# Moving every tile of a hybrid decoder block to another address: two unused tiles at the ends of SBUF

## The chip, the cores and the metric

The kernel runs on one core of one Trainium2 chip. The metric is the device time of one execution in microseconds (us). The times before come from three runs; one further execution was recorded by the hardware profiler.

## What is computed

One layer of a decoder block on `x` of 1,024 rows by 1,024 channels, all in float32. Cut to what matters here:

```python
xn = rmsnorm(x, norm1_g)
qa, ka, va, qr, kr, vr, gr, gate_a, gate_b = split(xn @ w_in)       # 1024 x 12800
o_a = dilated_attention(rmsnorm(qa), rmsnorm(ka), va)                # 12 heads of 128, 3 groups of 4
o_r = head_groupnorm(retention(qr, kr, vr)) * silu(gr)               # 4 heads, chunks of 128 rows
y = sigmoid(gate_a) * (o_a @ w_proj_a) + sigmoid(gate_b) * (o_r @ w_proj_b)
x = x + y @ w_out
x = x + square(relu(rmsnorm(x, norm2_g) @ w_up)) @ w_down            # 1024 x 4096 x 1024
```

The attention groups look at every first, fourth and sixteenth row back in a window; their three outputs per slot are mixed by their softmax denominators. Retention carries a state from chunk to chunk with a decay per head.

## The kernel before

The kernel is one program of 18,158 instructions. Its large matrix products keep float32 accuracy by splitting each operand into a high part and a remainder, both held in a rounded 32-bit type (`R` in the code, `F` is plain float32), and by three matmuls for each product of two tiles:

```python
def mm(x, y, start, stop):
    self.nc.tensor.matmul(ps, x, y, start=start, stop=stop, skip_group_check=not first)   # line 193
...
mm(xh, yh, first and i == 0, False)
mm(xh, yl, False, False)
mm(xl, yh, False, i == n - 1)
```

The first operand is the stationary one (128 x 128, loaded into TensorE ahead of the matmul), the second is streamed through it, 384 or 512 columns at a time. All 9,780 matmuls of `R` data stand on line 193 (in `Pipe.group`), 2,304 of 384 columns and 7,476 of 512. Splitting a tile takes one ScalarE copy (line 287) and one VectorE subtraction (line 288).

The work goes through these stages, one after the other, with TensorE's order written out by hand:

- Attention: for each of 12 heads, eight row blocks of 128 rows; each takes 24 matmuls of 384 columns (query, key and value together; the rows of the normalised input are stationary, the weights are streamed), then transposes (line 607), scores (532), transposed probabilities (545) and values (552) in plain float32 (`F`). The rest of a block runs some steps later through a list of due functions (`Pipe.at`), so that TensorE has other matmuls meanwhile. `acc` (line 554) takes the output of a block, 128 values in rows of 130.
- Input products: gates, retention's queries and keys, its output gate, in seven products for eight (Strassen), on halves of 512 columns; `wh`/`wl` are stationary, `xh`/`xl` streamed.
- Retention: four heads, eight chunks each, with values (line 193), scores (769), a state update (`kzh`, `kzl`) and outputs (`vh`, `Sh`, `qh`, `smh`), transposes at 780 and 825.
- Projections of both mixers, with operands and gates reloaded from DRAM.
- The output product, the second norm and the transposes of its rows (line 958).
- The up product (Strassen again), whose squared-ReLU result goes to DRAM (`h_d`), and the down product, which reads it back as `h`, `xh`, `xl` and adds eight partial results into `Yd` (line 1109).

Weights come in by one class, `Weights`, with three or four raw buffers and six pairs of split buffers (`wh0` to `wh5`, `wl0` to `wl5`), each 4,096 bytes per partition. All transfers are issued by SyncE.

Where a tile lies is decided by pools. A pool grows either from the left end of SBUF upwards or, with `side="right"`, from the right end downwards; pools open and close in the order of the code, and a tile starts at a multiple of 32 bytes. The first left pool is `const`, so its content shifts every later left tile:

```python
const = pool(ctx, "const", 1)
rawp = pool(ctx, "rawp", 1)
wp = pool(ctx, "wp", 1)
big = pool(ctx, "big", 4)
...
half = const.tile([P, 2], F, name="half")
ident = const.tile([P, P], F, name="ident")
```

With this, the built program has `half` at byte 16512 of each partition, `ident` at 16544, `raw0` at 17120, `wh0` at 29408, the first `xh` of `big` at 78560, and on the right `bias` of attention at 175840 and `qT` at 177888. The streamed operand of each of the 9,780 matmuls begins 96 bytes past a multiple of 128.

Of the kernel before, what the change touches and what calls it, by code (L numbers as in the profile page):

```python
# [10 lines left out]
F = mybir.dt.float32  # L11
# [6 lines left out]
P = 128  # L18
# [219 lines left out]
def hybrid_block(ctx: ExitStack, tc: tile.TileContext, a: dict, out: bass.AP):  # L238
# [3 lines left out]
    def pool(stack, name, bufs, side="left", **kw):  # L242
        return stack.enter_context(tc.tile_pool(name=name, bufs=bufs, side=side, reuse_waits="tile", **kw))

    const = pool(ctx, "const", 1)
    rawp = pool(ctx, "rawp", 1)
    wp = pool(ctx, "wp", 1)
    big = pool(ctx, "big", 4)
# [959 lines left out]
```

## Time and profile before

| | us |
|---|---|
| median of 3 runs | 2324.09 (2323.64 to 2328.1) |
| profiled execution | 2327.33 |
| its span | 2325.6 |
| TensorE matmuls busy | 2281.0 (98%) |
| TensorE weight loads busy | 1952.9 (84%) |
| VectorE / ScalarE / GpSimd busy | 1165.8 / 926.2 / 104.0 |
| mean granted TensorE clock | 0.995 |
| HBM traffic | 303.19 MB, 130 GB/s over the span |

The profile lists instructions with their start and length. A matmul's length goes from its start to its modelled end and overlaps the next one, so the pace is read from the distance between starts, or from a piece of many matmuls in the chain of work that ended last. Weight loads overlap matmuls too.

### The profile page before, as it was taken

How to read it: one execution, taken by the hardware profiler on the slowest of the kernel's cores; microseconds unless marked ns; L12 is line 12 of the kernel's file. 1: busy time of each engine (PE TensorE's matmuls, PEld its weight loads, DVE VectorE, ACT ScalarE, POOL GpSimd, SP SyncE). 2: the span in 40 equal slices, each digit the busy share in tenths (PEclk: the TensorE clock that was granted, in tenths of full speed). 3: DMA queues.
4: the chain of work that ended last, by engine and by line, in shares of the span. 5: the costliest groups of instructions: out<-in, count | busy, mean ns of one | idle time of the engine just before them, and what ended most of it. 6: DMA issues, size and time to landing. Idle time of an engine off the chain costs nothing. (4 is left out here: it accounts for less than half of the span.)

```text
span 2325.6 us, 29822 instructions
## 1 busy us (share of the span) xinstructions
PE 2281.0 (98%) x11060; PEld 1952.9 (84%) x11060; DVE 1165.8 (50%) x2356; ACT 926.2 (40%) x2078; POOL 104.0 (4%) x148
## 2 busy tenths in 40 slices
PE   8999999999999999989999999999999999999999
PEld 7999998998888888868888878888788888888887
DVE  6344445454644445557676752363855555233532
ACT  6444444445343333335455533122566666211010
POOL 1111111110000000000000000000000000000000
PEclk9999999999999999999999999999999999999999
DMA  4212322332233333363433385554254457733601
GB/s 140 82 55 74 105 63 78 96 105 91 68 112 112 117 113 109 100 187 104 123 113 100 104 273 180 164 171 163 83 173 166 167 169 271 288 127 133 234 28 73
DMA packets 186275, 303.19 MB, mean 130 GB/s; under 512 B 13457, under 2 KB 99601, under 8 KB 182034
## 3 DMA queue, kind: packets, MB, share of 16 engines
q1 hardware_dynamic: 186130, 301.29, 39.9%
q8 instruction: 87, 1.43, 0.3%
q14 instruction: 58, 0.48, 0.1%
HBM read 204.68 MB, written 96.57 MB: 130 GB/s over the span
## 5 line engine op out<-in xcount | busy, mean ns | idle before, releaser
L193 PE MATMUL mm<-wh,xh 128*128 128x384 f32 (+1 forms) x1536 | 605.1, 394 | 5.1 <-ACT wh L287 5.1
L193 PE MATMUL mm<-wh,xl 128*128 128x384 f32 (+1 forms) x1536 | 561.7, 366 | 2.4 <-DVE xl L288 2.1
L288 DVE TENSOR_TENSOR wl<-raw,wh 128x1024 fp32r<-128x1024 f32 (+2 forms) x282 | 306.6, 1092 | 423.1 <-ACT wh L287 420.1
L193 PE MATMUL mm<-wl,xh 128*128 128x384 f32 (+1 forms) x1344 | 486.6, 362 | 2.6 <-DVE wl L288 2.6
L287 ACT ACTIVATE wh<-raw 128x1024 fp32r<-128x1024 f32 (+2 forms) x282 | 267.2, 953 | 535.7 <-PE mm L193 272.1
L193 PEld LDWEIGHTS mm<-wh,xh 128*128 128x128 f32 x1536 | 291.5, 190 | 36.6 <-ACT wh L287 5.7
L193 PEld LDWEIGHTS mm<-wh,xl 128*128 128x128 f32 x1536 | 290.4, 189 | 35.5 <-DVE xl L288 3.4
L193 PE MATMUL mm<-xl,wh 128*128 128x512 f32 x848 | 309.7, 390 | 1.7 <-DVE xl L288 1.7
L193 PE MATMUL mm<-xh,wh 128*128 128x512 f32 x848 | 310.1, 390 | 0.0
L193 PE MATMUL mm<-xh,wl 128*128 128x512 f32 x720 | 280.7, 390 | 0.0
L193 PEld LDWEIGHTS mm<-wl,xh 128*128 128x128 f32 x1344 | 256.3, 191 | 24.8 <-DVE wl L288 3.1
L193 PE MATMUL ms<-xh,wh 128*128 128x512 f32 x604 | 238.6, 395 | 3.9 <-DVE s L888 3.8
L193 PE MATMUL ms<-xh,wl 128*128 128x512 f32 x604 | 235.4, 390 | 0.0
L193 PE MATMUL ms<-xl,wh 128*128 128x512 f32 x604 | 235.3, 390 | 0.0
L193 PEld LDWEIGHTS mm<-xl,wh 128*128 128x128 f32 x848 | 159.5, 188 | 35.2 <-DVE xl L288 2.1
L193 PEld LDWEIGHTS mm<-xh,wh 128*128 128x128 f32 x848 | 159.6, 188 | 33.0
L1109 DVE TENSOR_TENSOR Yd<-Yd,mm 128x512 f32<-128x512 f32 x112 | 76.9, 686 | 172.3 <-PE mm L193 172.0
L193 PEld LDWEIGHTS mm<-xh,wl 128*128 128x128 f32 x720 | 135.4, 188 | 28.1
L193 PEld LDWEIGHTS ms<-xh,wh 128*128 128x128 f32 x604 | 113.5, 188 | 30.1 <-DVE s L888 4.2
L193 PEld LDWEIGHTS ms<-xh,wl 128*128 128x128 f32 x604 | 113.4, 188 | 23.8
L193 PEld LDWEIGHTS ms<-xl,wh 128*128 128x128 f32 x604 | 113.5, 188 | 22.4
L539 ACT ACTIVATE pr<-s,acc 128x128 f32<-128x128 f32 (+1 forms) x96 | 43.1, 449 | 149.2 <-DVE acc L537 136.9
(187 smaller groups left out, 2756.4 us busy)
## 6 DMA issues: line engine op xcount, KB each, us to landing
h_d<-hs SPq DMA_DIRECT2D x64, 512.0 KB, 3.9
raw<-in_w_att SPq DMA_DIRECT2D x48, 384.0 KB, 3.9
raw<-in_w_up SPq DMA_DIRECT2D x32, 512.0 KB, 3.9
raw<-in_w_down SPq DMA_DIRECT2D x32, 512.0 KB, 4.4
xh<-h_d SPq DMA_DIRECT2D x12, 1024.0 KB, 7.1
xl<-h_d SPq DMA_DIRECT2D x12, 1024.0 KB, 8.7
sg_d<-sg SPq DMA_DIRECT2D x32, 256.0 KB, 2.0
raw<-in_w_rqk_q SPq DMA_DIRECT2D x16, 512.0 KB, 3.6
```

The lines of the kernel that those rows point to most:

```text
L193: self.nc.tensor.matmul(ps, x, y, start=start, stop=stop, skip_group_check=not first)
L287: nc.scalar.activation(dst_h, src, AF.Copy)
L288: nc.vector.tensor_tensor(dst_l, src, dst_h.bitcast(F), op=OP.subtract)
L539: nc.scalar.activation(st["p"][:, :n], s[:, :n], AF.Exp, bias=acc[:, b, DH:DH + 1], accum_out=acc[:, b, DH + 1:DH + 2])
L1109: nc.vector.tensor_tensor(Y[:, t, ns], Y[:, t, ns], pm, op=OP.add)
```

## The change

Two tiles are allocated and never used: one of 96 bytes per partition at the right end, the first of all right pools, and one of 32 bytes at the beginning of `const`.

```diff
+
     const = pool(ctx, "const", 1)
+    edge = pool(ctx, "edge", 1, "right")
+    edge.tile([P, 24], F, name="edge_r")
+    const.tile([P, 8], F, name="edge_l")
     rawp = pool(ctx, "rawp", 1)
```

In the built program every tile in a left pool moves up by 32 bytes and every tile in a right pool down by 96 (`raw0` to 17152, `wh0` to 29440, `xh` to 78592, `bias` to 175744, `qT` to 177792). No instruction, wait or order changes. The streamed operand of each of the 9,780 matmuls of line 193 then begins at a multiple of 128 bytes. Not every tile does: `ident`, `qk`, `s`, `junk`, `sm`, `kzh` and `kzl` begin 64 past a multiple, `half` 32 past one.

## The prediction

> **What bounds the kernel now.** I read the page first, for its busy shares, then the busy time by stage, then the chain of work that ended last, then the matmuls one by one.
>
> ```profile
> span 2325.6 us, 29822 instructions
> PE 2281.0 (98%) x11060; PEld 1952.9 (84%) x11060; DVE 1165.8 (50%) x2356; ACT 926.2 (40%) x2078; POOL 104.0 (4%) x148
> 0.00:520.00 520.00, 501.06 (x3021) 484.07 (x3022) 243.56 (x867) 232.01 (x895) 68.81 (x104) 0.99 0.30 89
> 520.00:1010.00 490.00, 488.40 (x2211) 405.21 (x2210) 240.86 (x355) 191.60 (x318) 3.37 (x4) 1.00 0.32 104
> 1010.00:1300.00 290.00, 280.80 (x1348) 231.48 (x1346) 200.84 (x465) 150.12 (x313) 22.50 (x27) 0.98 0.41 123
> 1300.00:1392.00 92.00, 86.14 (x390) 68.87 (x389) 60.03 (x102) 39.95 (x72) 3.81 (x5) 1.00 0.63 200
> 1623.00:1674.00 51.00, 46.04 (x231) 37.43 (x229) 42.95 (x77) 28.93 (x53) 4.64 (x7) 0.99 0.32 103
> 1674.00:1951.00 277.00, 277.00 (x1217) 228.41 (x1216) 157.99 (x211) 171.45 (x277) 0.00 (x0) 1.00 0.50 169
> 1392.18 230.52 PE mm L193 x1017
> 1960.35 9.54 DMA xl<-h_d
> 1973.62 348.17 PE mm L193 x1536
> ```
>
> The first two lines are the page's: TensorE is busy 98% of the span, VectorE half, ScalarE 40%. The six lines after them are stages (from:to, length, then busy time of PE, PEld, DVE, ACT, POOL, granted clock, DMA share, GB/s): attention, input products, retention, projections, output product with the second norm, up product. In the second and the last PE has practically no idle time; in attention it lacks 18.9 us, in retention 9.2, in the projections 5.9, in the norm stage 5.0. The last three lines are pieces of the chain (start, length, what). Two of them are nothing but matmuls of line 193: 1,017 in 230.52 us and 1,536 in 348.17 us, 226.67 ns from one to the next in both. So the kernel lasts as long as its matmuls need, and one number, the gap between two matmuls, sets it.
>
> That gap can be taken apart with the timeline of PE (start, length, engine, line, operation), where the granted clock falls to half for a few us:
>
> ```profile
> 233.28 0.52 PE L193 MATMUL mm<-wl,xh 128*128 128x384 f32 x1
> ...
> 235.84 0.52 PE L193 MATMUL mm<-wh,xh 128*128 128x384 f32 x1
> 236.59 0.34 PE L193 MATMUL mm<-wh,xh 128*128 128x384 f32 x1
> ...
> 237.98 0.33 PE L193 MATMUL mm<-wh,xl 128*128 128x384 f32 x1
> 1674.50 0.63 PE L193 MATMUL mm<-xl,wh 128*128 128x512 f32 x1
> ...
> 1676.21 0.63 PE L193 MATMUL mm<-xh,wl 128*128 128x512 f32 x1
> 1118.51 0.60 PE L769 MATMUL ms<-rqT,rkT 128*128 128x128 f32 x4
> ```
>
> At half clock eight gaps of 384 columns take 2.56 us, 320 ns each, and four gaps of 512 columns take 1.71 us, 427 ns each: 0.833 ns a column and nothing beside it. At full clock a column would be 0.417 ns, so 384 columns are 160 ns and 512 are 213.3 ns. The rows say 1.39 / 8 = 173.8 ns and 226.67 ns. Both are 13.3 ns too long, whatever the width: 32 columns' time. It is a cost of every matmul that streams R data at full clock, hidden at half clock. The last row is of matmuls that take F data, four passes of 128 columns in 0.60 us. Less the 0.27 us that one pass takes to its end (273 ns in rows shown below), three gaps are 0.33 us, about 109 ns each. Two column times for each of 128 columns are 106.7, so there only 2 to 3 ns are over.
>
> **The change part by part.** The built program of the changed kernel has the same 18,158 instructions in the same order on every engine, with the same waits and the same shapes. Nothing is added: the two tiles are never written or read. Only addresses differ. Tiles in pools that grow from the left move up by 32 bytes, tiles in right pools down by 96. All 9,780 matmuls of line 193 stream an operand that begins 96 bytes past a multiple of 128 before, and at a multiple of 128 after (7,476 of 512 columns, 2,304 of 384). Their stationary operands go from 96 to 0 as well, save 168 (32 to 64). The words of the change are not true of all: `ident`, `qk`, `s`, `sm`, `kzh` begin at 64 past a multiple, `half` at 32. None of these is streamed as R data.
>
> So every term is a price per access. 32 columns are 128 bytes. If the stream is fetched in pieces of 128 bytes, 512 columns from an offset of 96 touch 17 pieces, 17 x 32 = 544 column times = 226.67 ns; 384 columns touch 13, 416 column times = 173.3 ns. Both are the rows above. From an offset of 0 they touch 16 and 12. At half clock, and with F data that take two column times each, the fetch would have time to spare, and there the cost is missing. This is an inference; no R matmul of this kernel streams from another offset, so the trace cannot show it.
>
> **Price of a matmul.** It is bounded by 0 saved (the cost has nothing to do with the address) and 13.3 ns saved (213.3, no cost left, as at half clock); what it could lose stands under rival (4). I take 2.5 ns of start cost as left, the middle of what the F passes show, hence 215.8 ns and 10.8 ns saved, nearer to the upper end because the cost is 32 columns to the digit. The Trainium skill ("TensorE: Matmul & The Clock Gate", section "Back-to-back issue gap") gives columns / 2.4 + 2.5 ns for a warm matmul, an estimate of 215.8 ns at 512. The trace does not agree: 226.67 ns. By that rule nothing but those 215.8 ns is proper to a matmul and some 106 us of the kernel are another cost; by the row alone it could all be proper and the sum would be nothing.
>
> **Other engines at nothing.** Accesses of other engines show no price for the offset:
>
> ```profile
> L554 ACT ACTIVATE acc<-ms 128x128 f32<-128x128 f32 x96 | 26.3, 274 | 28.4 <-PE ms L552 27.8
> L600 ACT ACTIVATE V<-mm 128x128 f32<-128x128 f32 x96 | 25.9, 270 | 0.0
> L430 PE MATMUL tr<-ident,oa 128*128 128x128 f32 x32 | 4.8, 272 | 0.0
> L825 PE MATMUL tr<-ident,on 128*128 128x128 f32 x128 | 19.3, 273 | 0.8 <-DVE on L804 0.7
> L769 PEld LDWEIGHTS ms<-rqT,rkT 128*128 128x128 f32 x128 | 19.2, 190 | 2.7
> ```
>
> `acc` is written in rows of 520 bytes, so the 96 writes of line 554 go through every offset in steps of 8 bytes, and cost 274 ns; those of line 600, all at 96, cost 270. `oa` lies at 0 for 24 of 32 transposes, `on` always at 96: 272 and 273 ns. Transfers move the same bytes. The weight load, 190 ns in the row, does not become the bound either: the passes of line 769 have one each and follow each other every 109 ns, under the 162.5 ns that 384 columns would take.
>
> **What lies on the path.** The matmuls of line 193 by stage (length, PE, PEld, clock, DMA share, GB/s):
>
> ```profile
> 0.00:520.00 520.00, 479.08 (x2227) 380.64 (x2228) 0.99 0.30 89
> 520.00:1010.00 490.00, 485.25 (x2108) 391.99 (x2108) 1.00 0.32 104
> 1010.00:1300.00 290.00, 264.12 (x1070) 197.99 (x1068) 0.98 0.41 123
> 1300.00:1392.00 92.00, 83.31 (x348) 63.97 (x347) 1.00 0.63 200
> 1392.00:1623.00 231.00, 230.81 (x1019) 190.83 (x1018) 1.00 0.53 173
> 1623.00:1674.00 51.00, 42.46 (x169) 30.37 (x169) 0.99 0.32 103
> 1674.00:1951.00 277.00, 277.00 (x1215) 228.41 (x1216) 1.00 0.50 169
> 1951.00:1973.60 22.60, 22.33 (x99) 18.19 (x98) 1.00 0.88 312
> 1973.60:2325.60 352.00, 348.18 (x1537) 287.99 (x1535) 1.00 0.41 149
> ```
>
> Four stages are PE alone (520, 1392, 1674, 1973.6): 2,108 + 1,019 + 1,215 + 1,537 = 5,879 matmuls x 10.8 ns = 63.5 us, all kept, since the busiest other engine there, ScalarE in the up product (171 of 277 us), still has room if the stage gets 13 us shorter. Attention: 2,227 x 10.8 = 24.1 us, retention 1,070 x 10.8 = 11.6 us. There PE idles 4% and 3%, so some steps are set by the chain over the vector and scalar engines, which stays as long; I keep four fifths, 19.3 and 9.3. Projections and norm stage: 517 x 10.8 = 5.6 us, half kept, 2.8, because transfers set part of them. At 1951 the chain runs through the transfer of `xl` from `h_d` (9.54 us), under which the 99 matmuls merely wait longer: 1.1 us, nothing kept. Sum 63.5 + 19.3 + 9.3 + 2.8 = 94.9 us.
>
> The profiled execution took 2327.33 us (its span and 1.7 us around it), 3.2 over the median of the runs, 2324.09. 2327.3 - 94.9 = 2232.4, or 2229 against the median.
>
> **The rivals.**
>
> (1) The 13.3 ns are a fixed cost of an R matmul and the address is nothing to it. Then all else is the same and the time stays at 2324. For it: no offset but 96 occurs, and the rows of ScalarE and of the F passes show no address anywhere. The Trainium skill ("SBUF — State Buffer", "Specifications (TRN2)") gives lines of 16 bytes; 96 is a whole number of those, so by that page an operand at 96 is aligned already and the time would not move. Against it: the cost is 32 columns to the digit at two widths, and vanishes where the fetch has twice the time, which a start cost of the array would not. Chance 9%.
>
> (2) The gap falls, but the stages with idle time keep their length, because their chains over VectorE and ScalarE take PE's place as the bound: only the 63.5 us are kept, 2324.1 - 63.5 = 2261. For it: their idle time; against it: in attention PE is still busy 501 of 520 us, so most steps are its own. Chance 10%.
>
> (3) Half of the 13.3 ns is address, half start cost: 6.7 ns x 9,780 = 65 us, less a tenth, 2266. Against it: nothing in the rows speaks for two causes. Chance 5%.
>
> (4) Slower: left and right pools move against each other by 128 bytes. Where the weights lie left and the streamed operand right (four of seven products of 21 input units, three of seven of 16 up units, 12 matmuls each, 1,584), streams and loads may begin to meet. The trace has stretched gaps in retention, where vector and scalar engines touch more tiles at a time:
>
> ```profile
> 1115.73 0.39 PE L193 MATMUL ms<-vh,kzh 128*128 128x512 f32 x1
> ...
> 1117.12 0.40 PE L193 MATMUL mm<-wh,xh 128*128 128x512 f32 x1
> ```
>
> Six gaps in 1.39 us are 232 ns, 5 over 226.67. If those 1,584 went there, with no gain from alignment, that is +8 us, 2332. It decides from 2.9 ns a gap, 4.6 us. Against it: each pool's tiles keep their mutual distances. Chance 4%.
>
> **How the numbers follow.** The forecast has 72%: 2229, its own range 2189 (13.3 ns saved by all 9,780, 130 us, and retention's 5 ns of stretch gone for its 1,070) to 2245 (10 ns saved, and half kept in every stage with idle time). All cases but (1) and (4) lie under 2275, 87%; that is the range, 2189 to 2275. A measurement of this kernel can tell about 0.2%, 4.6 us, from no change. Faster 0.87, same 0.09, slower 0.04.
>
> **What would show it.** In the profile after, the piece of 1,536 matmuls in the chain should last 331 us instead of 348.17, the 1,017 some 219.5 instead of 230.52, gaps of 384 columns in attention should be near 162.5 ns, and the rows at half clock should still say 320 and 427. The activations of line 554 should not move. PE's idle time should grow from 44.6 us to about 55. If the 1,536 still last 348, rival (1) is right; if they last 331 and the sum is under 70 us, rival (2). The forecast is wrong in its mechanism if the gap changes by anything but some ten ns at both widths.

## The result: 0.5% slower, where a streamed operand lies right and the weights left

The changed kernel takes 2335.53 us (2334.66 to 2338.39, four runs) against 2323.86 before, 1.0048 times as long (95% interval 1.0031 to 1.0066). The forecast was 2229. Its profiled execution took 2338.39 us; the page of after, and the pieces of the chain of work that ended last which stand for the two quoted before:

```profile
span 2336.6 us, 29822 instructions
PE 2292.7 (98%) x11060; PEld 1951.2 (84%) x11060; DVE 1165.8 (50%) x2356; ACT 926.3 (40%) x2078; POOL 104.1 (4%) x148
1396.65 234.19 PE mm L193 x1017
1984.70 348.19 PE mm L193 x1536
```

The span is 11.0 us longer, and PE's busy time 11.7. VectorE and ScalarE are as busy as before to 0.1 us. The 1,536 matmuls of the down product, forecast at 331 us, last 348.19 after 348.17: 226.7 ns a gap at offset 96 and at offset 0. The 1,017 of the later projections and the output product became slower, 234.19 us after 230.52. By stage, cut at the same work as before (length, then busy PE, PEld, DVE, ACT, POOL, clock, DMA share, GB/s):

```profile
0.00:519.50 519.50, 499.50 (x3021) 482.44 (x3022) 244.18 (x867) 231.96 (x894) 68.95 (x104) 0.99 0.30 89
519.50:1016.10 496.60, 495.34 (x2210) 405.25 (x2209) 240.77 (x355) 191.79 (x319) 3.37 (x4) 1.00 0.32 103
1016.10:1304.60 288.50, 279.37 (x1348) 230.72 (x1347) 200.74 (x465) 149.87 (x313) 22.50 (x27) 0.99 0.41 124
1396.40:1631.00 234.60, 234.60 (x1023) 191.25 (x1021) 87.75 (x111) 55.67 (x81) 0.81 (x2) 1.00 0.53 169
1681.80:1962.20 280.40, 279.64 (x1217) 227.89 (x1216) 158.32 (x212) 171.99 (x278) 0.00 (x0) 1.00 0.49 167
1984.60:2336.60 352.00, 348.27 (x1537) 288.14 (x1535) 121.62 (x160) 42.06 (x50) 0.00 (x0) 1.00 0.41 149
```

The six rows are attention, input products, retention, the later projections with most of the output product, up product and down product. Input products 496.6 us after 490.0, projections and output product 234.6 after 231.0, up product 280.4 after 277.0: +13.6 us. Retention gives back 1.5 and attention 0.5. Where inside a stage, the groups of matmuls by shape tell, first of before, then of after (count, busy us and mean ns of one; a length runs some 163 ns beyond the gap):

```profile
L193 PE MATMUL ms<-xh,wl 128*128 128x512 f32 x604 | 235.4, 390 | 0.0
L193 PE MATMUL ms<-xl,wh 128*128 128x512 f32 x604 | 235.3, 390 | 0.0
L193 PE MATMUL mm<-wh,h 128*128 128x512 f32 x256 | 79.1, 389 | 0.0
```

```profile
L193 PE MATMUL ms<-xh,wl 128*128 128x512 f32 x604 | 238.5, 395 | 0.0
L193 PE MATMUL ms<-xl,wh 128*128 128x512 f32 x604 | 238.0, 394 | 0.7 <-DVE xl L292 0.7
L193 PE MATMUL mm<-wh,h 128*128 128x512 f32 x256 | 79.1, 389 | 0.0
```

`ms` takes the products that mostly stream a right-hand `xh` or `xl` (a row names the streamed operand first, then the weights); they grew by 4 to 5 ns each on the mean. `mm<-wh,h` streams left weights and grew by nothing. One such product of 12 matmuls in the timeline of before, then one of after (start of its first matmul and of the next product's first):

```profile
696.13 0.39 PE L193 MATMUL ms<-xh,wh 128*128 128x512 f32 x1
...
698.85 0.39 PE L193 MATMUL mm<-xh,wh 128*128 128x512 f32 x1
```

```profile
702.39 0.40 PE L193 MATMUL ms<-xh,wh 128*128 128x512 f32 x1
...
705.18 0.40 PE L193 MATMUL mm<-xh,wh 128*128 128x512 f32 x1
```

2.72 us became 2.79: 226.7 ns a gap, then 232.5. This is rival (4) of the prediction. What left and right had in common before, and lost, is seen in the built programs. Before, the split weights, the normalised input and the right-hand streams all began at the same place modulo 256 bytes (at 224); only operands of retention stood elsewhere. After, left ones are at 0, right ones at 128. Of the 9,293 successive pairs of R matmuls, 260 had stream and next weights at unequal places modulo 256 before (all but one in retention), and 2,376 after: 1,584 in the input and up products, 383 in the projections, 185 in the output product, 224 in retention.

### The profile page after: what moved, and what is told of

It is laid out like the page before. It is cut to its first block, busy times and chain, and to the rows that moved or that the text cites. A ratio compares the mean times of both kernels' runs of the same rounds, so it can differ in the third digit from the quotient of the medians.

```text
span 2336.6 us, 29822 instructions
## 1 busy us (share of the span) xinstructions
PE 2292.7 (98%) x11060; PEld 1951.2 (84%) x11060; DVE 1165.8 (50%) x2356; ACT 926.3 (40%) x2078; POOL 104.1 (4%) x148
```

## The experiments

Theory PAIR: a matmul streams slower where the streamed operand and the weights loaded meanwhile do not lie a multiple of 256 bytes apart. Rival ALIGN: what counts is where an operand begins by itself. Rival OTHERS: the streams meet other engines or transfers. Each timed run is compared with the kernel before on the same chip (2322.86 us beside the first three whole kernels, 2320.05 beside the last three). The gaps of whole kernels given below are means over pairs of successive R matmuls in the trace, with the addresses of the built program put to them in order; gaps over 260 ns, in which TensorE waited, are left out.

### The pair by itself

The probe runs 48 R matmuls per group, with nothing else busy, and slices both operands out of two tiles at chosen offsets:

```diff
+            for i in range(count):
+                s, w = sd[i % len(sd)] // size, wd[i % len(wd)] // size
+                nc.tensor.matmul(ps[:, :n], we[kind][:, w:w + P], st[kind][:, s:s + n], start=i == 0,
+                                 stop=i == count - 1)
```

> A probe of the disputed cost alone: it computes none of the block (its output is zeros and one row block of copied data). TensorE runs groups of 48 matmuls, nothing else is busy; each group has one offset of the streamed operand and one of the weights, in bytes, and its own output tile, named for them (letters for digits: a=0 to j=9; streambci = stream at 128, weights at 0). Theory PAIR (a matmul streams slower where the streamed operand and the weights that are loaded meanwhile differ in address by something else than a multiple of 256 bytes): groups both* and streamcfg (256), streamfbc (512) at 226.7 ns a gap, streambci (128) and weightbci at about 232 to 233, streambjc (192) about 232. Rival ALIGN (what counts is where an operand begins by itself): both* groups differ among each other, and streambci equals weight at 0 and stream at 128 only by the stream. Rival OTHERS (streams meet the accesses of other engines or of transfers): all groups of R data alike, 226.7 ns. If 13.3 ns are a fixed cost of an R matmul, no group of 512 columns is under 226.7 ns; bf16 groups (half*) would show whether it belongs to R data: 215.8 ns by the formula of the Trainium skill (TensorE: Matmul & The Clock Gate, Back-to-back issue gap), an estimate.

The timeline of PE, one row for a group (start, length of all 48):

```profile
20.36 11.68 PE L101 MATMUL bothe<-st,we 128*128 128x512 f32 x48 [0.69 <-ACT o L103]
32.78 11.37 PE L101 MATMUL bothbg<-st,we 128*128 128x512 f32 x48 [0.75 <-ACT o L103]
44.90 11.17 PE L101 MATMUL bothdc<-st,we 128*128 128x512 f32 x48 [0.75 <-ACT o L103]
68.74 11.18 PE L101 MATMUL bothjg<-st,we 128*128 128x512 f32 x48 [0.75 <-ACT o L103]
80.67 11.18 PE L101 MATMUL bothbci<-st,we 128*128 128x512 f32 x48 [0.75 <-ACT o L103]
129.32 11.47 PE L101 MATMUL streamdc<-st,we 128*128 128x512 f32 x48 [0.75 <-ACT o L103]
141.54 11.28 PE L101 MATMUL streamge<-st,we 128*128 128x512 f32 x48 [0.75 <-ACT o L103]
165.78 11.43 PE L101 MATMUL streambci<-st,we 128*128 128x512 f32 x48 [0.75 <-ACT o L103]
214.62 11.22 PE L101 MATMUL streamcfg<-st,we 128*128 128x512 f32 x48 [0.75 <-ACT o L103]
323.47 11.43 PE L101 MATMUL weightbci<-st,we 128*128 128x512 f32 x48 [0.75 <-ACT o L103]
383.78 8.61 PE L101 MATMUL colsdiebya<-st,we 128*128 128x384 f32 x48 [0.75 <-ACT o L103]
402.39 6.02 PE L101 MATMUL colscfgbya<-st,we 128*128 128x256 f32 x48 [0.64 <-ACT o L103]
470.66 10.52 PE L101 MATMUL halffbcbya<-hst,hwe 128*128 128x512 bf16 x48 [0.75 <-ACT o L103]
493.19 10.52 PE L101 MATMUL halffbcbybci<-hst,hwe 128*128 128x512 bf16 x48 [0.74 <-ACT o L103]
```

Both operands at 32, 96 or 128 take the same 11.17 to 11.18 us, so among multiples of 32, where every tile begins, the offset by itself is nothing: there ALIGN falls. Below that it is something: both at 4 take 11.68 us (237.7 ns a gap) and both at 16 take 11.37 (231.1), as ALIGN and not PAIR would have it; no tile of the kernel begins there. A stream 128 past the weights takes 11.43, and so do weights 128 past the stream. 256 apart is back at 11.22 (its first gaps were longer). From the thirteenth matmul on, the starts in the trace are this far apart on the mean:

| stream past weights, modulo 256 bytes | 0 | 32 | 64 | 96 | 128 | 160 | 192 | 224 |
|---|---|---|---|---|---|---|---|---|
| gap, 512 columns of R, ns | 226.7 | 233.4 | 228.9 | 233.4 | 232.4 | 234.3 | 233.3 | 233.4 |

No R group of 512 columns is under 226.7, at any address. At 384 columns it is 173.3 and at 256 columns 120.0 for equal addresses: a column's time each and 13.3 ns. At 128 columns it is 111.6, so the sum does not go on. The price of a distance of 128 shrinks with the width: 5.7 ns at 512 columns, 2.7 at 384 (176.0), none at 256 (118.7) or 128 (111.7). bf16 operands take 215.8 ns, at differences of 0 and of 128 alike. So the 13.3 ns belong to R data, not to the offset, and rival (1) is right about them. The Trainium skill's formula ("TensorE: Matmul & The Clock Gate", "Back-to-back issue gap"), an estimate of 215.8 ns, agrees with the bf16 groups and not with R data.

Two more groups take turns: weights at 0 and 128 under a stream at 0 give 232.2 ns on the mean (233.7 where the next weights are at 128, 230.6 where they are at 0), a stream at 0 and 128 over weights at 0 gives 229.9. The mean of 226.7 and 232.4 is 229.5, so with changing weights a price for each pair alone does not add up; whether the next weights or a matmul's own are what counts is not settled by them.

### The change with another distance, and the distance without the change

```diff
+    edge = pool(ctx, "edge", 1, "right")
+    edge.tile([P, 56], F, name="edge_r")     # 224 bytes where the change has 96
+    const.tile([P, 8], F, name="edge_l")
```

> The whole kernel, left pools up by 32 bytes as in the change, right pools down by 224 instead of 96: the streamed operands all begin at multiples of 128 as in the change, but left and right tiles stand to each other as before, modulo 256. PAIR: 2324 us, all of the loss gone, products with a right-hand stream back at 226.7 ns a gap. ALIGN: 2335, as the change. OTHERS: no number, near 2335.

Measured 2323.29 us, ratio 1.0002 (0.9993 to 1.0011), and the piece of the projections and the output product in the chain is back:

```profile
1388.34 230.52 PE mm L193 x1017
```

All streams begin at multiples of 128, as in the change, and nothing is lost. Now the reverse, right pools down by 128 and all else in place:

```diff
+    edge = pool(ctx, "edge", 1, "right")
+    edge.tile([P, 32], F, name="edge_r")     # 128 bytes, nothing on the left
```

> The whole kernel, left pools where they were, right pools down by 128: every operand at 96 past a multiple of 128 as before the change, left and right 128 apart from before. PAIR: 2335 us, as the change (1,584 matmuls with a right-hand stream at about 233 ns). ALIGN: 2324. OTHERS: no number, near 2335 if the meeting is with right-hand tiles.

Measured 2335.85 us, 1.0058 (1.0045 to 1.0071): the whole loss with every stream at 96 past a multiple of 128. The piece again:

```profile
1394.71 234.19 PE mm L193 x1017
```

ALIGN predicted the other way in both. Half of the change alone:

```diff
+    const.tile([P, 8], F, name="edge_l")     # left pools up by 32 bytes, right ones in place
```

> The whole kernel, half of the change alone: left pools up by 32 bytes, right pools where they were; left operands at multiples of 128, right ones at 96, their difference 32 less than a multiple of 256. PAIR: over 2324, by how much depends on the price at a difference of 32, which the probe measures: at the price of 128, 2334. ALIGN: between 2324 and 2335, since only left operands change.

2339.87 us, 1.0074 (1.0061 to 1.0086): +17 us, more than the change. The probe has 233.4 ns at this difference (224) against 232.4 at 128. The whole kernel's gaps at 224 are 233.5 on the mean of 1,993.

### A larger dose, and a price that did not carry over

128 unused bytes between the split weights and the normalised input part most of the left-hand pairs as well:

```diff
+    gap = pool(ctx, "gap", 1)
+    gap.tile([P, 32], F, name="gap")
     big = pool(ctx, "big", 4)
```

> The whole kernel of before with 128 unused bytes between the pools of the split weights and of the normalised input: 4,715 more matmuls of 512 columns and 1,923 of 384 have stream and next weights 128 apart. PAIR at the probe's prices (5.7 ns at 512 columns, 2.7 at 384): 26.9 + 5.2 = +32 us, 2355; +27 if attention, whose matmuls are interrupted every few, is as slow already. ALIGN (offset by itself): no operand leaves its place relative to 128, so 2323. OTHERS: no number.

2346.12 us, 1.0110 (1.0096 to 1.0123): +26 us, at the lower of the two numbers. The down product now pays as well, 233.3 ns a gap:

```profile
1983.69 358.41 PE mm L193 x1536
```

Attention paid nothing: its gaps of 384 columns are 175.8 ns after 175.5 (means of those in the trace that no F matmul touches). Before, with equal addresses, they were already as long as the probe's with unequal ones, 176.0. Then a difference of 64, cheap in the probe:

```diff
+    edge = pool(ctx, "edge", 1, "right")
+    edge.tile([P, 48], F, name="edge_r")     # 192 bytes, nothing on the left
```

> The whole kernel of before, right pools down by 192 and the left ones as they were: 1,999 more matmuls have the stream 64 past the next weights modulo 256, where the probe's gap is 228.9 (2.2 ns more), and 217 more 192 past them (6.6 ns more, instead of 128 for some). PAIR: +4.4 + 1.4 - 0.5 = +5 us, 2328. A rule that only equal or unequal counts: +12, 2335. ALIGN: right operands at 32 past a multiple of 128 instead of 96, no number.

2333.05 us, 1.0052 (1.0038 to 1.0066): +13 us, not +5. The rule of equal or unequal named +12, but its price for a pair is not what the gaps show. The pairs at 64 have 230.1 ns on the mean of 2,021, 2.7 more than the equal ones before, 5.5 us in all. The rest is in the pairs at equal addresses, which went from 227.4 to 229.0 ns, 4,834 of them, 7.9 us. The first ten or so gaps after each such product are stretched (224 to 236 ns), and from the eleventh on they are 226.7. In the changed kernel, after products with a distance of 128, only the first three are stretched (231 to 233 ns). The next probe shows the same settling.

### What an interruption does

> A second probe; it computes none of the block. Groups of 48 R matmuls of 512 columns, weights and stream at the same address modulo 256, or the stream 128 on (names with shift). What it asks: where the 13.3 ns come from that every R matmul of 512, 384 and 256 columns has, and a bf16 one has not. Theory LOAD (the stream and the load of the next weights share the reading of the memory, the load takes 32 column times from the stream in the best case): with weights of 64 instead of 128 columns (rowssixtyfour) the gap falls to about 220, with 32 (rowsthirtytwo) to about 217; in mix, where R and bf16 matmuls alternate, the R matmul whose successor's weights are bf16 falls under 226.7. Rival STREAM (the cost is the R stream's own): rows* stay at 226.7, R in mix stays at 226.7 and bf16 in mix at 215.8. Theory PHASE (after a matmul of F data the two readers need some matmuls to fall into step, and until then gaps are stretched even at equal addresses): broken, with one F matmul after every 12, lies clearly over 226.7, about 230. Rival PAIR alone: broken at 226.7 but for the interruption. busy and busyshift have ScalarE and VectorE copying in SBUF all the time: 226.7 and 232.4 if no other engine counts, more if OTHERS plays a part.

The probe alters a group in one thing at a time: fewer weight columns (rows), an F matmul after every 12 (broken), ScalarE and VectorE copying meanwhile (busy); shift is a stream 128 past the weights.

```diff
+                if broken and i % 12 == 0 and i:
+                    nc.tensor.matmul(extra[:, :P], pwe[:, :P], pst[:, :P], start=True, stop=True)
...
+                    nc.tensor.matmul(ps[:rows], we[:, :rows], st[:, d // 4:d // 4 + 512], start=i == 0,
+                                     stop=i == COUNT - 1)
```

Timeline rows, and the busy times of both busy groups (PE, PEld, DVE, ACT):

```profile
20.28 11.17 PE L77 MATMUL full<-st,we 128*128 128x512 f32 x48 [0.69 <-ACT o L79]
32.20 11.43 PE L77 MATMUL fullshift<-st,we 128*128 128x512 f32 x48 [0.75 <-ACT o L79]
44.38 11.26 PE L77 MATMUL rowssixtyfour<-st,we 128*64 128x512 f32 x48 [0.75 <-ACT o L79]
56.37 11.23 PE L77 MATMUL rowssixtyfourshift<-st,we 128*64 128x512 f32 x48 [0.74 <-ACT o L79]
68.34 11.31 PE L77 MATMUL rowsthirtytwo<-st,we 128*32 128x512 f32 x48 [0.74 <-ACT o L79]
80.38 11.26 PE L77 MATMUL rowsthirtytwoshift<-st,we 128*32 128x512 f32 x48 [0.74 <-ACT o L79]
107.46 3.02 PE L77 MATMUL broken<-st,we 128*128 128x512 f32 x12
110.32 0.38 PE L73 MATMUL extra<-pst,pwe 128*128 128x128 f32 x2
120.25 3.03 PE L77 MATMUL brokenshift<-st,we 128*128 128x512 f32 x12
123.11 0.39 PE L73 MATMUL extra<-pst,pwe 128*128 128x128 f32 x2
141.98 11.17 PE L77 MATMUL busy<-st,we 128*128 128x512 f32 x48 [0.75 <-ACT o L79]
167.22 11.43 PE L77 MATMUL busyshift<-st,we 128*128 128x512 f32 x48 [0.75 <-ACT o L79]
```

```profile
142.00:153.00 11.00, 11.00 (x48) 8.91 (x48) 10.72 (x9) 10.68 (x11) 0.00 (x0) 1.00 0.00 0
167.40:178.40 11.00, 11.00 (x48) 8.78 (x47) 10.72 (x9) 10.68 (x11) 0.00 (x0) 1.00 0.00 0
```

With two engines busy 97% of the time the groups keep 11.17 and 11.43 us, so these engines are no part of it; OTHERS falls for ScalarE and VectorE (transfers were not tried). After an F matmul, 12 R matmuls take 2.86 us until the next F matmul starts, and 2.87 to 2.88 at unequal addresses, where 12 times 5.7 ns would be 0.07 more. The first of these gaps is 314 ns, the others 231 on the mean at equal addresses. In the starts of `full`, the gaps after a first one of 337 are 236, 228, 233 and 231 ns, then 226 to 227 to the end: R matmuls take some gaps to reach 226.7, and an interruption costs that anew. PHASE's number, about 230, is borne out, and it fits that attention, interrupted every few matmuls, did not care for the distance. LOAD is not borne out: with 64 or 32 weight columns gaps do not fall, they rise to 229.9 and 231.6 ns. STREAM, that they stay at 226.7, misses too. With so few weight columns the distance costs nothing either: the shifted groups have 229.3 and 230.5 ns, no more than the others. In mix, an R and a bf16 matmul take 460 ns together, more than 226.7 + 215.8, so alternating the two types costs something by itself and the group decides nothing.

### All pairs equal

The built programs say which pairs were unequal before: the 260 of retention, because two statistics tiles there (`st`) take 128 bytes between them and two tiles of mixing weights (`w`, no operand of these matmuls) 192. Widening both brings stream and next weights of every pair of R matmuls to the same place modulo 256:

```diff
-        w = p2b.tile([P, 6, 4], F, name="w")
+        w = p2b.tile([P, 8, 4], F, name="w")
...
-                    st = p2.tile([P, 12], F, name="st")
+                    st = p2.tile([P, 32], F, name="st")
```

> The whole kernel of before with two small tiles of retention widened (a statistics tile from 12 to 32 floats per row, a weight tile of the slot mix from 6 to 8), so that all 9,780 R matmuls have stream and next weights at the same address modulo 256; before, 260 in retention had differences of 64, 128 and 192. PAIR alone, with every stretched gap of retention an echo of those: some 1,070 gaps of 231 go to 227, -4.5 us, 2318. PHASE: only the 260 gain, 5 ns each, -1.3 us, 2321 to 2322, not to be told from no change. OTHERS: no change.

2317.39 us against 2320.05, ratio 0.9990 (0.9981 to 0.9998). That is some 2.7 us faster than the kernel before, between the -4.5 and the -1.3 expected, and the interval only just leaves out no change. Retention, cut at the same matmuls, in before and then in this kernel:

```profile
1009.90:1300.00 290.10, 280.90 (x1348) 231.56 (x1346) 200.84 (x465) 150.22 (x313) 22.50 (x27) 0.98 0.41 123
```

```profile
1005.40:1293.00 287.60, 277.64 (x1347) 230.96 (x1346) 200.34 (x465) 150.26 (x313) 21.82 (x27) 0.98 0.41 124
```

290.1 us became 287.6; in the kernel with 224 bytes on the right, whose pairs stand as before, it was 290.3. A stage's length differs between executions by itself (attention, where no pair changed, is 516.2 us in this trace after 520.0), so the gaps are the firmer sign: its some 940 gaps without a wait fell from 231.2 to 228.6 ns on the mean, 2.4 us in all. They did not fall to 226.7, as fits the F matmuls between them, after which the gaps are stretched anew.

## Why the prediction was wrong

- **Identical programs, everything in the addresses: right.** So was that no other engine changes: VectorE and ScalarE kept their busy times, and TensorE remained the bound.
- **Price of a matmul: the step that failed.** It took 10.8 of the 13.3 ns for the cost of an offset of 96. The measured saving is 0: the 13.3 ns are there at 32, 96 and 128 alike and belong to R data, and what the change did cost, 5.4 ns on 2,116 more pairs, goes by the distance between stream and weights, which the sum left out and only rival (4) had. The inference rested on two rows, 226.67 and 173.8 ns, that fit 17 and 13 pieces of 128 bytes (226.67 and 173.3), and just as well a constant. The two widths could not tell these apart, because both are a whole number of such pieces. The prediction said that no R matmul streams from another offset, and still gave the inference 72%.
- **The rows at half clock and of F data** were read as a fetch with time to spare. They bear out as much that the cost is one of the R stream at full clock, which rival (1) said at 9%. The probe's bf16 groups (215.8 ns) and its offsets (226.7 at 32, 96 and 128) decided for it.
- **What lies on the path, 94.9 us:** every term was a count times 10.8 ns, and fell with it.
- **Rival (4), given 4%, was what happened:** right place, left weights against a right-hand stream, and nearly the right price, 5 ns for 5.4 (232.8 ns on the mean of the unequal pairs after, 227.4 of the equal ones before). It counted 1,584 matmuls and left out the projections and the output product. By the built programs 2,116 more pairs are unequal, x 5.4 ns = 11.4 us; it named +8. The equal pairs became 0.56 ns longer on the mean, 2.8 us, as the first ones after an unequal product are stretched, and attention and retention gave back 2, for which no run shows a cause. The objection, "each pool's tiles keep their mutual distances", missed that a matmul takes its two operands from two pools. The stretched gaps of retention that the prediction quoted, and put beside busy vector and scalar engines, were the effect itself: by the built program `vh` and `kzh` stand 192 bytes apart modulo 256 there, and the probe's two busy engines changed nothing.
- **The Trainium skill on 16-byte lines** ("SBUF — State Buffer", "Specifications (TRN2)"), by which 96 is aligned already, agrees for addresses that a tile can have: 11.17 us at 32, 11.18 at 96 and 128. It does not agree at 16, a whole line as well, where the probe took 11.37. Its page "TensorE: Matmul & The Clock Gate" ("Step-by-step: what each phase is for") says that loading the next weights takes no reading bandwidth from the running matmul. For bf16 the runs agree, 215.8 ns at both distances. For R data the gap does depend on the distance of the two, 226.7 or 232.4 ns; that it is the load which takes this time is not shown.

What stays open: where the 13.3 ns of an R matmul come from, why a settled pace takes several gaps to reach, and whether it is the load of the next weights that the stream meets. That the distance of the two operands makes the difference is shown by the runs, which put the loss in and took it away with nothing else changed; that they meet in the reading of the memory is argued from it. The groups with 64 and 32 weight columns, where the distance cost nothing, speak for a part of the load, but their equal gaps rose as well.

## What to carry to other kernels

Before padding for alignment, ask of which two accesses the alignment is: here, with all tiles at multiples of 32, only the distance between streamed operand and weights counted, and tiles of opposite pools have a distance that nobody chose. Look in the built program at the addresses of operands that are used together, and keep them a multiple of 256 bytes apart for 32-bit R data streamed 512 columns at a time in long runs, where it was worth 0.5% to 1.1% of this kernel; small odd tiles in one of the pools break it. A constant that fits a round number of columns is no evidence of a cause until one size or offset has been moved against it.

## What the runs showed of the hardware

A matmul of R data has a gap of one column time each and 13.3 ns (226.7 at 512 columns, 173.3 at 384, 120.0 at 256; 111.6 at 128 does not fit), and bf16 has 215.8 at 512. Where stream and weights begin at multiples of 32 and are not a multiple of 256 bytes apart, R matmuls of 512 columns stretch to 229 to 234 ns; for bf16 a distance of 128 is nothing. With both operands at 4 or at 16, the gap was 237.7 and 231.1 ns. After an interruption, R matmuls at equal addresses have a long first gap (314 ns after an F matmul, 334 to 341 at the start of a group) and then from four to ten of 224 to 240 ns until they run at 226.7 again.
